# The opening of a two-layer decoder kernel: gain row spread by TensorE, fused scaling on VectorE, loads in halves, identity transposes first

## The chip, the cores and the metric

The kernel runs on one core of one Trainium2 chip. The time is the device time of one execution in microseconds (us). A core has TensorE (PE in the profile; PEld is its weight load), VectorE (DVE), ScalarE (ACT), GpSimd (POOL) and SyncE (SP, which here only issues DMAs). Each engine has its own instruction queue, taken in order; engines wait for each other by semaphores. TensorE writes its results into PSUM, eight banks of 128 x 512 fp32; all else lies in SBUF.

## The reference

Two layers over x of 512 rows by 1024 features, fp32. Layer 0 has dilated-window attention as its mixer, layer 1 a gated linear recurrence; a gated convolutional feed-forward follows each. Every sub-layer stands between two root-mean-square norms. The opening computes the first norm and the first product with the attention weights:

```python
def rms_norm(x, g):
    xf = x.astype(jnp.float32)
    y = xf * lax.rsqrt(jnp.mean(xf * xf, axis=-1, keepdims=True) + RMS_EPS)
    return (y * g.astype(jnp.float32)).astype(x.dtype)

for layer in range(DEPTH):
    h = rms_norm(x, norm_mix_pre[layer])
    h = dilated_attention_mixer(h, attn_w_qkv[j], ...)   # or rglru_mixer; both begin with h @ w
    x = x + rms_norm(h, norm_mix_post[layer])
    h = rms_norm(x, norm_ffn_pre[layer])
    h = conv_ffn(h, ...)
    x = x + rms_norm(h, norm_ffn_post[layer])
```

The kernel makes each of these products of three passes in the format fp32r: a value is split into hi (rounded) and lo (the remainder), and hi x hi, hi x lo and lo x hi are summed in PSUM.

## The kernel before

The 512 rows of x lie as four row tiles of 128 in `x_sb`, 1024 features wide. Weights come from HBM in chunks of 1 MB (`load`, on SP's queue, three `raw` buffers). `pump` takes one unit of a chunk, half of it, and issues the split: per 128 x 512 piece one ScalarE copy to `whi` (L146) and one VectorE subtraction to `wlo` (L147). Eight split units may live. `take` returns a unit for use and pumps if it isn't there yet; `tick`, called between matmul groups, pumps too and runs the side jobs of attention. The order of every engine's queue is the order in which the Python code issues instructions; nothing reorders it.

The opening stands at the end of the kernel function. L951 issues a root on one column, so that ScalarE loads its table. Then come the loads, all on SP: row tile 0 of x (512 KB), the gain row read 128 times into all partitions (`gain`, 512 KB, L142), weight chunk 0, tile 1, chunk 1, tiles 2 and 3.

`first_norm` (L304) is a generator with two steps. The first multiplies each half of a tile by the gain (L312: on VectorE for tile 0, on GpSimd for tiles 1 to 3) and squares and sums each half on ScalarE (L315). The second adds the two sums (L318), makes 1/root with one correction step (L319 to L325: one ScalarE root, the rest on VectorE) and scales the halves (L328 and L331 on VectorE, L330 on ScalarE). `transposed` (L293) brings a scaled tile into the feature-major `hT`: per half four TensorE transposes into a PSUM bank (L297), a ScalarE copy to the hi part (L301), a VectorE subtraction to the lo part (L302).

The first matmul work is `values` (L595) of attention: for each row tile t, 24 matmuls (8 feature blocks, three passes, L246 to L248) of a 128 x 128 block of `hT` with a 512-wide block of weights, into a bank `v`. It calls `start` (L962) through `begin`: before tile 0 it issues the whole norm and transposes of tile 0, the four units of chunks 0 and 1, the whole norm of tile 1 and the first step of tiles 2 and 3; before tile 1 the transposes of tile 1 and the second step of tiles 2 and 3; after tile 1's matmuls the transposes of tiles 2 and 3. The two first results are copied out of PSUM after that (L623).

Behind this, attention goes on with queries and keys of a head pair (`feat_tiles`), and side jobs build the bias tables: for each of three groups a small fp32 matmul (`bv`, L563), a copy, a DMA to HBM (`rowv`, L565), a DMA that copies it 128 times (`skew`, 1.5 MB, L566). The scores of a head (L651) wait for a load from it (`toe`, L579). These three DMAs are on GpSimd's queue.

The main lines are:

```python
(nc.gpsimd if t else nc.vector).tensor_tensor(xs[t][i], xh, halves(g)[i], op=ALU.mult)   # L312
nc.scalar.activation(junk, xh, AF.Square, accum_out=ss[:, c : c + 1])                     # L315
nc.scalar.activation(hi, raw, AF.Copy)                                                    # L146
nc.vector.tensor_tensor(lo, raw, hi.bitcast(F32), op=ALU.subtract)                        # L147
```

Of the kernel before, what the change touches and what calls it, by code (L numbers as in the profile page):

```python
# [18 lines left out]
P = 128  # L19
S = 512  # L20
D = 1024
# [55 lines left out]
def kernel(  # L77
# [42 lines left out]
    def nm(s):  # L120
        uid[0] += 1
        return f"{s}{uid[0]}"
# [7 lines left out]
    def small(cols, s="s"):  # L130
        return sp.tile([P, cols], F32, tag=f"s{cols}", name=nm(s))
# [32 lines left out]
    def pump(limit=2):  # L164

        for _ in range(limit):
            i = state["cv"]
            if not pieces and i < state["dma"]:
                pieces.extend((i, j, u) for j, u in enumerate(parts_of(plan[i][0], raws.pop(i))))
                state["cv"] += 1  # L170
            if pieces and state["live"] < W_UNITS:
                i, j, raw = pieces.pop(0)
                hi, lo = (
                    wp.tile([P] + list(raw.shape[1:]), F32R, tag=t, name=nm("w" + t)) for t in ("hi", "lo")
                )
# [66 lines left out]
    def w_rows(w, r0):  # L242
        plan.append(("rows", 2, D, [(w[r0 : r0 + 256, :].rearrange("(k p) c -> p k c", p=P), 2)]))

    def mm3(dst, l, r, start, stop):
        mm(dst, l[0], r[0], start=start, stop=False)  # L246
        mm(dst, l[0], r[1], start=False, stop=False)  # L247
        mm(dst, l[1], r[0], start=False, stop=stop)  # L248

    def rms(parts, before=None, after=None):  # L250

# [17 lines left out]
    def root_table():  # L269

        one = small(1)
        nc.scalar.activation(one, ident[:, 0:1], AF.Sqrt)

    def halves(ap):
        return [ap[:, 0:512], ap[:, 512:1024]]

    def new_hT():
        return tuple(htp.tile([P, KD, S], F32R, tag=f"hT{i}", name=nm(f"hT{i}")) for i in range(2))
# [11 lines left out]
        yield wait  # L290
        transposed(t, xs, hT)

    def transposed(t, xs, hT):  # L293
        for i in range(2):
            ps = psum("tr")
            for k in range(4):
                nc.tensor.transpose(ps[:, k * P : (k + 1) * P], xs[i][:, k * P : (k + 1) * P], ident)  # L297
# [3 lines left out]
            nc.scalar.activation(hi, ps3, AF.Copy)  # L301
            nc.vector.tensor_tensor(lo, ps3, hi.bitcast(F32), op=ALU.subtract)  # L302

    def first_norm(tiles, g, scaled):  # L304

        n = len(tiles)
        ss, v, y, q = small(4), small(2), small(2), small(2)
        xs = {t: [gen(s="xs") for _ in range(2)] for t in tiles}
        for i in range(2):
            for j, t in enumerate(tiles):  # L310
                xh = halves(x_sb[:, t, :])[i]
                (nc.gpsimd if t else nc.vector).tensor_tensor(xs[t][i], xh, halves(g)[i], op=ALU.mult)  # L312
                junk = gen(s="junk")
                c = 2 * i + j
                nc.scalar.activation(junk, xh, AF.Square, accum_out=ss[:, c : c + 1])  # L315
        yield
        v, y, q = v[:, :n], y[:, :n], q[:, :n]
        nc.vector.tensor_tensor(v, ss[:, 0:n], ss[:, 2 : 2 + n], op=ALU.add)  # L318
        nc.vector.tensor_scalar(v, v, 1.0 / D, EPS, op0=ALU.mult, op1=ALU.add)  # L319
        nc.scalar.activation(y, v, AF.Sqrt)  # L320
        nc.vector.reciprocal(y, y)
        nc.vector.tensor_tensor(q, y, y, op=ALU.mult)
        nc.vector.tensor_tensor(q, q, v, op=ALU.mult)
        nc.vector.tensor_scalar(q, q, -0.5, 1.5, op0=ALU.mult, op1=ALU.add)
        nc.vector.tensor_tensor(y, y, q, op=ALU.mult)  # L325
        for j, t in enumerate(tiles):
            if t == 1:
                nc.vector.tensor_scalar(xs[t][0], xs[t][0], y[:, j : j + 1], None, op0=ALU.mult)  # L328
            else:
                nc.scalar.activation(xs[t][0], xs[t][0], AF.Copy, scale=y[:, j : j + 1])  # L330
# [213 lines left out]
    def attention(hT, post, pre):  # L544
# [50 lines left out]
        def values(vs, permute, midway=None):  # L595

            if permute:
                vd = dp.tile([S, 512], F32, name=f"vrows{len(vrows)}")
                vrows.append(vd)
            ids = [chunk(), chunk()]  # L600
            banks = {}
            begin = first_tiles[0] if first_tiles else None
            for t in range(4):
                if begin and t < 2:
                    begin(t)
                banks[t] = psum("v")
                for k in range(KD):
                    mm3(
                        banks[t],
                        [h[:, k, t * P : (t + 1) * P] for h in hT],  # L610
                        [v[:, k % 2, :] for v in take(ids[k // 4], k // 2 % 2)],
                        k == 0,
                        k == KD - 1,
                    )
                    if t == 3 and k % 4 == 3:
# [319 lines left out]
    for layer in range(2):  # L935
# [23 lines left out]
    scaled = {}  # L959
    parts = [first_norm(tiles, g, scaled) for tiles in ([0], [1], [2, 3])]  # L960
# [54 lines left out]
```

## Time and profile before

| what | value |
|---|---|
| median of 3 runs | 1498.67 us (1498.09 to 1500.18) |
| the profiled execution | 1498.71 us |
| its span | 1496.9 us |
| mean granted TensorE clock over the span | 0.997 |
| first instruction of TensorE | 10.35 us |
| VectorE's wlo (L147), all 504 of the weights | 328.1 us, 697 ns mean |
| GpSimd's gain products (L312), six | 9.5 us, 1602 ns mean |
| waiting of TensorE for L330 before its first transpose | 10.4 us |

The span is the time from the first to the last instruction in the profile; the execution's time has a little around it. In a timeline or chain a row begins with the start in us from the span's beginning and the length; "x8" merges eight instructions of a line; "out<-in" names the tiles with their buffer numbers left out. A bracket gives how long the engine sat idle before, and what ended that. In the table of groups the two numbers behind the bar are the busy time in us and the mean of one in ns. A matmul's length includes its way through the array, so the rate is read from the distance between starts.

### The profile page before, as it was taken

Reading aid. Unit: us, or ns where it says so; the run is one execution under the profiler, and the core shown is the slowest. Engines: PE = TensorE matmul, PEld = TensorE weight load, DVE = VectorE, ACT = ScalarE, POOL = GpSimd, SP = SyncE. Lnnn points to the kernel's source line nnn. Section 1 sums busy time; section 2 is a strip of 40 time slices with the busy share of each in tenths; the row PEclk is TensorE's granted clock in tenths of the full one; section 3 lists DMA queues with packets and bytes.
Section 4 is the critical chain, followed back from the end, with each engine's and each line's share of the span. In section 5 each row is a group of like instructions: output and inputs, shape, how many; then the busy total and the mean of one; then the engine's idle time right before and its main releaser. Section 6 shows DMA issues by size and latency. Waiting matters only on the chain.

```text
span 1496.9 us, 18111 instructions
## 1 busy us (share of the span) xinstructions
PE 1474.0 (98%) x7083; PEld 1237.8 (83%) x7083; DVE 795.3 (53%) x1612; ACT 633.7 (42%) x1287; POOL 43.7 (3%) x73
## 2 busy tenths in 40 slices
PE   6999999999999999999999999999999999999998
PEld 4788888888888898888888888988898888888886
DVE  6434334343434586555555336877876555565333
ACT  5334333333334554333344334579554333344321
POOL 3111000000000000000000000000000000000000
PEclk9999999999999999999999999999999999999999
DMA  6543222423334233323233231342233232323301
GB/s 215 184 164 98 92 88 85 133 100 125 107 121 137 95 110 119 106 87 111 85 113 113 85 113 43 99 142 84 85 99 113 92 105 87 110 85 116 109 1 56
DMA packets 116101, 157.64 MB, mean 105 GB/s; under 512 B 5087, under 2 KB 97463, under 8 KB 116016
## 3 DMA queue, kind: packets, MB, share of 16 engines
q1 hardware_dynamic: 111120, 145.24, 29.3%
q0 software_dynamic: 4896, 11.26, 2.3%
q8 instruction: 55, 0.90, 0.3%
q14 instruction: 30, 0.25, 0.0%
HBM read 150.14 MB, written 11.05 MB: 108 GB/s over the span
## 4 chain that ended last, share of the span: by engine, by line
PE 88%; ACT 5%; DVE 4%; DMA 2%; issue 1%; SPq 0%; POOL 0%; DVEq 0%; ACTq 0%; POOLq 0%
PE ps L246 17%; PE ps L248 17%; PE ps L247 17%; PE acc L248 7%; PE acc L246 7%; PE acc L247 7%; PE v L246 3%; PE v L247 3%; PE v L248 3%; DVE wlo L147 2%; DVE xb L838 1%; ACT whi L146 1%; PE S L714 1%; PE tr L297 1%; PE O L772 1%; PE O L699 1%
## 5 line engine op out<-in xcount | busy, mean ns | idle before, releaser
L246 PE MATMUL ps<-hT,whi 128*128 128x512 f32 (+1 forms) x1376 | 518.5, 377 | 0.0
L248 PE MATMUL ps<-hT,wlo 128*128 128x512 f32 (+1 forms) x1376 | 515.2, 374 | 0.0
L247 PE MATMUL ps<-hT,whi 128*128 128x512 f32 (+1 forms) x1376 | 515.1, 374 | 0.0
L147 DVE TENSOR_TENSOR wlo<-raw,whi 128x512 fp32r<-128x512 f32 x504 | 328.1, 697 | 270.3 <-ACT whi L146 270.1
L146 ACT ACTIVATE whi<-raw 128x512 fp32r<-128x512 f32 x504 | 285.2, 623 | 135.0 <-PE acc L248 120.9
L246 PEld LDWEIGHTS ps<-hT,whi 128*128 128x128 f32 x1376 | 259.1, 188 | 47.0 <-ACT qk L590 0.6
L248 PEld LDWEIGHTS ps<-hT,wlo 128*128 128x128 f32 x1376 | 259.0, 188 | 46.5
L247 PEld LDWEIGHTS ps<-hT,whi 128*128 128x128 f32 x1376 | 259.1, 188 | 45.6
L517 DVE SCALAR_TENSOR_TENSOR u<-ps,cols,u 128x511 f32<-128x511 f32 x192 | 143.8, 749 | 140.4 <-ACT u L513 137.0
L248 PE MATMUL acc<-whi,alo 128*128 128x512 f32 x512 | 199.4, 389 | 1.0 <-DVE alo L147 1.0
L246 PE MATMUL acc<-whi,ahi 128*128 128x512 f32 x512 | 200.0, 391 | 0.0
L247 PE MATMUL acc<-wlo,ahi 128*128 128x512 f32 x512 | 199.2, 389 | 0.0
L513 ACT ACTIVATE u<-ps,cols 128x512 f32<-128x512 f32 x96 | 74.8, 780 | 209.9 <-PE ps L248 209.9
L248 PEld LDWEIGHTS acc<-whi,alo 128*128 128x128 f32 x512 | 96.1, 188 | 21.4 <-DVE alo L147 1.4
L246 PEld LDWEIGHTS acc<-whi,ahi 128*128 128x128 f32 x512 | 96.1, 188 | 19.7
L247 PEld LDWEIGHTS acc<-wlo,ahi 128*128 128x128 f32 x512 | 96.1, 188 | 19.6
L246 PE MATMUL v<-whi,hT 128*128 128x512 f32 x192 | 78.3, 408 | 0.0
L247 PE MATMUL v<-wlo,hT 128*128 128x512 f32 x192 | 76.5, 398 | 1.4 <-DVE wlo L147 1.4
L248 PE MATMUL v<-whi,hT 128*128 128x512 f32 x192 | 76.3, 398 | 0.5 <-DVE hT L302 0.5
L528 ACT ACTIVATE u<-u 128x512 f32<-128x512 f32 x48 | 30.3, 632 | 80.6 <-DVE u L517 80.6
L651 DVE CUSTOM_DVE_ANT_0 L<-S,toe 128x128 f32<-128x128 f32 (+1 forms) x96 | 25.2, 320 | 53.4 <-DMA toe<-skew 22.7
L590 ACT ACTIVATE qk<-ps 128x512 f32<-128x512 f32 x24 | 14.3, 597 | 88.7 <-PE ps L248 76.9
(169 smaller groups left out, 1028.5 us busy)
## 6 DMA issues: line engine op xcount, KB each, us to landing
raw<-in_ffn_w_up_dram SPq DMA_DIRECT2D x48, 1024.0 KB, 5.2
raw<-in_attn_w_qkv_dram SPq DMA_DIRECT2D x28, 1024.0 KB, 5.1
raw<-in_ffn_w_down_dram SPq DMA_DIRECT2D x24, 1024.0 KB, 4.9
raw<-in_attn_w_qkv_dram SPq DMA_DIRECT2D x16, 512.0 KB, 4.9
raw<-in_lru_w_in_dram SPq DMA_DIRECT2D x8, 1024.0 KB, 5.4
skew<-rowv POOLq DMA_DIRECT2D x3, 1536.0 KB, 12.3
vrows<-v SPq DMA_DIRECT2D x16, 256.0 KB, 2.8
vp<-vrows SPq DMA_DIRECT2D x16, 256.0 KB, 4.0
```

Of the source, the lines that this page charges most:

```text
L146: nc.scalar.activation(hi, raw, AF.Copy)
L147: nc.vector.tensor_tensor(lo, raw, hi.bitcast(F32), op=ALU.subtract)
L246: mm(dst, l[0], r[0], start=start, stop=False)
L247: mm(dst, l[0], r[1], start=False, stop=False)
L248: mm(dst, l[1], r[0], start=False, stop=stop)
L297: nc.tensor.transpose(ps[:, k * P : (k + 1) * P], xs[i][:, k * P : (k + 1) * P], ident)
L513: nc.scalar.activation(u, ps, AF.Identity, scale=cc[:, j : j + 1], bias=cc[:, 48 + j : 49 + j])
L517: nc.vector.scalar_tensor_tensor(u[:, d:], ps[:, : S - d], wc, u[:, d:], op0=ALU.mult, op1=ALU.add)
L528: nc.scalar.activation(u, u, AF.Gelu_apprx_tanh)
L651: nc.vector.tensor_tensor_reduce(dst, ps, bias, scale=1.0, scalar=3 * NEG, op0=ALU.add, op1=ALU.max, accum_out=mx)
L699: mm(po[:, a * P : (a + 1) * P], pts[a, j], vtile(v, a - 1 + j, h % 4), start=j == js[0], stop=j == 1)
L714: mm(ps[:, c], q[hh][:, c], k[hh][:, c], start=True, stop=True)
```

## The change

The gain row is no longer read 128 times by a DMA. The new `first_gain` loads it into one partition (two DMAs of 2 KB on ScalarE's queue), multiplies it on TensorE by a column of ones (K = 1, fp32) into two PSUM banks and copies these to `g` on VectorE. Twelve transposes of the identity into an unused bank stand before and twelve after these two matmuls.

Row tile 0 of x and chunks 0 and 1 are loaded in two halves each; the SP order is tile 0, chunk 0, tile 1, chunk 1, tiles 2 and 3. The root for the table is issued after `first_gain`.

`first_norm` no longer multiplies by the gain on its own: a fused VectorE instruction per half computes x times the scale times the gain, for all tiles. The second half of tile 0 is squared and summed on VectorE. In `start`, tile 1's second step and tiles 2 and 3's first step move from before tile 0's matmuls to before tile 1's; the second step of tiles 2 and 3 moves to after tile 1's matmuls. The four weight units are interleaved differently with tile 0's transposes and tile 1's squares.

In `values`, tile 0's six matmuls of a unit are sorted by pass (hi x hi of both blocks first). For all other tiles the order is as before.

```diff
+WARM = 12
...
-            nc.sync.dma_start(raw[:, :, at : at + n] if kind == "value" else raw[:, at : at + n, :], src)
+            if i < 2:
+                for k in (0, 2):
+                    nc.sync.dma_start(raw[:, k : k + 2, :], src[:, k : k + 2, :])
+            else:
+                nc.sync.dma_start(raw[:, :, at : at + n] if kind == "value" else raw[:, at : at + n, :], src)
...
-    def transposed(t, xs, hT):
-        for i in range(2):
+    def transposed(t, xs, hT, parts=(0, 1)):
+        for i in parts:
...
-    def first_norm(tiles, g, scaled):
+    def first_norm(tiles, g):
...
-        for i in range(2):
-            for j, t in enumerate(tiles):
-                xh = halves(x_sb[:, t, :])[i]
-                (nc.gpsimd if t else nc.vector).tensor_tensor(xs[t][i], xh, halves(g)[i], op=ALU.mult)
+        for j, t in enumerate(tiles):
+            for i, h in enumerate(halves(x_sb[:, t, :])):
+                acc = (ss, s1)[i][:, j : j + 1]
                 junk = gen(s="junk")
-                c = 2 * i + j
-                nc.scalar.activation(junk, xh, AF.Square, accum_out=ss[:, c : c + 1])
-        yield
+                if t == 0 and i:
+                    nc.vector.tensor_tensor_reduce(
+                        junk, h, h, scale=1.0, scalar=0.0, op0=ALU.mult, op1=ALU.add, accum_out=acc
+                    )
+                else:
+                    nc.scalar.activation(junk, h, AF.Square, accum_out=acc)
+        nc.vector.tensor_scalar(b, ss, 1.0 / D, EPS, op0=ALU.mult, op1=ALU.add)
+        yield xs
+        nc.vector.scalar_tensor_tensor(v, s1, 1.0 / D, b, op0=ALU.mult, op1=ALU.add)
         nc.scalar.activation(y, v, AF.Sqrt)
...
         for j, t in enumerate(tiles):
-            if t == 1:
-                nc.vector.tensor_scalar(xs[t][0], xs[t][0], y[:, j : j + 1], None, op0=ALU.mult)
-            else:
-                nc.scalar.activation(xs[t][0], xs[t][0], AF.Copy, scale=y[:, j : j + 1])
-            nc.vector.tensor_scalar(xs[t][1], xs[t][1], y[:, j : j + 1], None, op0=ALU.mult)
-        scaled.update(xs)
+            for i, h in enumerate(halves(x_sb[:, t, :])):
+                nc.vector.scalar_tensor_tensor(
+                    xs[t][i], h, y[:, j : j + 1], halves(g)[i], op0=ALU.mult, op1=ALU.mult
+                )
+        yield xs
...
+                for u in range(4):
+                    W = take(ids[u // 2], u % 2)
+                    steps = [(k, a, b) for k in (2 * u, 2 * u + 1) for a, b in PASSES]
+                    if begin and t == 0:
+                        steps.sort(key=lambda s: PASSES.index(s[1:]))
...
+    def first_gain(src):
+
+        g = cp.tile([P, D], F32, tag="gain", name=nm("gain"), bufs=2)
+        row = [gen(s="row") for _ in range(2)]
+        for r, h in zip(row, halves(src)):
+            nc.scalar.dma_start(r[0:1, :], h)
+        one = gen(s="one")
+        nc.vector.memset(one[0:1, :P], 1.0)
+        warm = psum("warm")
+        for _ in range(WARM):
+            nc.tensor.transpose(warm[:, :P], ident, ident)
+        for r, h in zip(row, halves(g)):
+            ps = psum("gain")
+            mm(ps, one[0:1, :P], r[0:1, :], start=True, stop=True)
+            nc.vector.tensor_copy(h, ps)
+        for _ in range(WARM):
+            nc.tensor.transpose(warm[:, :P], ident, ident)
+        return g
+
+    hT = new_hT()
+    for i in range(2):
+        c = slice(i * 512, (i + 1) * 512)
+        nc.sync.dma_start(x_sb[:, 0, c], x[0, 0:P, c])
+    g = first_gain(norm_mix_pre[0:1, :])
     root_table()
-    hT = new_hT()
-    nc.sync.dma_start(x_sb[:, 0, :], x[0, 0:P, :])
-    g = gain(norm_mix_pre, 0, nc.sync)
+    load()
     for t in range(1, 4):
-        if t < 3:
+        nc.sync.dma_start(x_sb[:, t, :], x[0, t * P : (t + 1) * P, :])
+        if t == 1:
             load()
-        nc.sync.dma_start(x_sb[:, t, :], x[0, t * P : (t + 1) * P, :])
...
         if t == 0:
-            for _ in parts[0]:
-                pass
+            next(norm_of[0])
+            xs = next(norm_of[0])
             pump(1)
-            transposed(0, scaled[0], hT)
+            transposed(0, xs[0], hT, (0,))
             pump(1)
-            pump(2)
-            for _ in parts[1]:
-                pass
-            next(parts[2])
+            transposed(0, xs[0], hT, (1,))
+            pump(1)
+            next(norm_of[1])
+            pump(1)
         elif t == 1:
-            transposed(1, scaled[1], hT)
-            next(parts[2], None)
+            transposed(1, next(norm_of[1])[1], hT)
+            next(norm_of[2])
         else:
-            transposed(2, scaled[2], hT)
-            transposed(3, scaled[3], hT)
+            xs = next(norm_of[2])
+            transposed(2, xs[2], hT)
+            transposed(3, xs[3], hT)
```

More of the change, by code (lines that the diff above doesn't have):

```diff
@@ L243, in w_rows @@
         plan.append(("rows", 2, D, [(w[r0 : r0 + 256, :].rearrange("(k p) c -> p k c", p=P), 2)]))
+    PASSES = [(0, 0), (0, 1), (1, 0)]
     def mm3(dst, l, r, start, stop):
-        mm(dst, l[0], r[0], start=start, stop=False)
-        mm(dst, l[0], r[1], start=False, stop=False)
-        mm(dst, l[1], r[0], start=False, stop=stop)
+        for n, (a, b) in enumerate(PASSES):
+            mm(dst, l[a], r[b], start=start and n == 0, stop=stop and n == 2)
     def rms(parts, before=None, after=None):
@@ L302, in transposed @@
             nc.vector.tensor_tensor(lo, ps3, hi.bitcast(F32), op=ALU.subtract)
[L304 removed]
+    def first_norm(tiles, g):
         n = len(tiles)
[L307 removed]
+        ss, b, v, y, q = (small(2)[:, :n] for _ in range(5))
+        s1 = small(2)[:, :n]
         xs = {t: [gen(s="xs") for _ in range(2)] for t in tiles}
[L309 to L312 removed]
+        for j, t in enumerate(tiles):
+            for i, h in enumerate(halves(x_sb[:, t, :])):
+                acc = (ss, s1)[i][:, j : j + 1]
                 junk = gen(s="junk")
[L314 to L319 removed]
+                if t == 0 and i:
[7 more added lines that the diff above has]
+        nc.vector.scalar_tensor_tensor(v, s1, 1.0 / D, b, op0=ALU.mult, op1=ALU.add)
         nc.scalar.activation(y, v, AF.Sqrt)
         nc.vector.reciprocal(y, y)
[L322 to L323 removed]
+        nc.vector.tensor_tensor(q, y, v, op=ALU.mult)
+        nc.vector.tensor_tensor(q, q, y, op=ALU.mult)
         nc.vector.tensor_scalar(q, q, -0.5, 1.5, op0=ALU.mult, op1=ALU.add)
@@ L606, in values @@
                 banks[t] = psum("v")
[L607 to L615, printed above, removed]
+                for u in range(4):
[3 more added lines that the diff above has]
+                        steps.sort(key=lambda s: PASSES.index(s[1:]))
+                    for k, a, b in steps:
+                        mm(
+                            banks[t],
+                            hT[a][:, k, t * P : (t + 1) * P],
+                            W[b][:, k % 2, :],
+                            start=(k, a, b) == (0, 0, 0),
+                            stop=(k, a, b) == (KD - 1, 1, 0),
+                        )
+                    if t == 3 and u % 2:
                         done(2)
@@ L959 @@
-    scaled = {}
-    parts = [first_norm(tiles, g, scaled) for tiles in ([0], [1], [2, 3])]
+    norm_of = {t: first_norm(tiles, g) for t, tiles in ((0, [0]), (1, [1]), (2, [2, 3]))}
     def start(t):
         if t == 0:
-            for _ in parts[0]:
-                pass
+            next(norm_of[0])
+            xs = next(norm_of[0])
             pump(1)
-            transposed(0, scaled[0], hT)
+            transposed(0, xs[0], hT, (0,))
             pump(1)
-            pump(2)
-            for _ in parts[1]:
-                pass
-            next(parts[2])
+            transposed(0, xs[0], hT, (1,))
+            pump(1)
+            next(norm_of[1])
+            pump(1)
```

## The prediction

> **What bounds the kernel now.** I read the page first.
>
> ```profile
> span 1496.9 us, 18111 instructions
> PE 1474.0 (98%) x7083; PEld 1237.8 (83%) x7083; DVE 795.3 (53%) x1612; ACT 633.7 (42%) x1287; POOL 43.7 (3%) x73
> ```
>
> TensorE is the bound over the span. The change leaves every matmul of the layers in place, so it can win or lose only what TensorE waits, or does at half rate, in the opening. I take as its end the first matmul of row tile 2. The chain of waits (start, length, work, in us) says who sets that time:
>
> ```profile
> 1.19 5.43 DMA gain<-in_norm_mix_pre_dram
> 6.73 1.29 DVE xs L312 x2
> 9.52 0.72 ACT xs L330
> 10.79 2.40 DVE wlo L147 x2
> 14.31 8.04 DVE wlo L147 x6
> 23.93 0.49 DVE xs L328
> 24.46 1.48 PE tr L297 x8
> 73.96 9.89 DMA toe<-skew
> ```
>
> First it is the 512 KB broadcast of the gain row, then VectorE: wlo alone holds the chain for 10.4 us. From 24.46 TensorE holds it. The timeline (start, length, engine, line, work, in brackets the idle time before) shows why wlo is slow:
>
> ```profile
> 11.38 2.94 POOL L312 TENSOR_TENSOR xs<-x_sb,gain 128x512 f32<-128x512 f32 x2 [7.49 <-DMA x_sb<-in_x_dram]
> 15.29 6.52 POOL L312 TENSOR_TENSOR xs<-x_sb,gain 128x512 f32<-128x512 f32 x4 [0.97 <-DMA x_sb<-in_x_dram]
> 36.83 2.50 DVE L147 TENSOR_TENSOR wlo<-raw,whi 128x512 fp32r<-128x512 f32 x4 [0.47 <-ACT whi L146]
> ```
>
> Six wlo take 8.04 us (1.34 each) beside GpSimd's gain products; four take 2.50 (0.62 each) when GpSimd is still. The third view is TensorE's rate, from the timeline and from the busy time by stretch (its PEclk, the granted clock, is the third number from the end):
>
> ```profile
> 14.86 0.63 PE L247 MATMUL v<-wlo,hT 128*128 128x512 f32 x1
> 15.29 0.63 PE L248 MATMUL v<-whi,hT 128*128 128x512 f32 x1
> 29.20 0.39 PE L246 MATMUL v<-whi,hT 128*128 128x512 f32 x1
> 29.43 0.39 PE L247 MATMUL v<-wlo,hT 128*128 128x512 f32 x1
> 25.00:26.00 1.00, 1.00 (x7) 0.71 (x5) 0.19 (x1) 0.80 (x4) 0.00 (x0) 0.52 1.07 380
> ```
>
> A 512-column matmul starts every 0.43 us early on and every 0.23 us later. The granted clock falls to 0.52 again after the gap before 24.46 (for the first matmuls the column has no record, so I go by spacing).
>
> **The change part by part.** I follow four stages; "before" is this profiled execution.
>
> Stage 1, up to the first scaling (9.52 before). Its rows:
>
> ```profile
> 1.03 0.29 POOL masks.py:199 TENSOR_SCALAR_AFFINE_SELECT ident<-ident 128x128 f32<-128x128 f32 x1
> 7.94 0.15 DVE L318 TENSOR_TENSOR s<-s 128x1 f32<-128x1 f32 x1
> 10.38 1.94 PE L297 MATMUL tr<-ident,xs 128*128 128x128 f32 x8 [10.38 <-ACT xs L330]
> 50.83 0.81 PE L563 MATMUL bv<-oh,rb 33*8 33x384 f32 x2
> 51.67 0.55 DVE L564 COPY bv<-bv 8x384 f32<-8x384 f32 x1 [2.53 <-PE bv L563]
> L592 DVE COPY qk<-ps 128x512 f32<-128x512 f32 x24 | 16.6, 691 | 63.0 <-PE ps L248 63.0
> 83.99 0.29 DVE L651 CUSTOM_DVE_ANT_0 L<-S,toe 128x128 f32<-128x128 f32 x1 [13.27 <-DMA toe<-skew]
> 84.20 0.42 DVE L651 CUSTOM_DVE_ANT_0 L<-S,toe 128x256 f32<-128x256 f32 x1
> rb<-in_rel_bias_dram POOLq DMA_DIRECT2D x1, 3.0 KB, 6.3
> DMA to landing us min/median/max: 3.7/10.5/12.4
> ```
>
> The identity is ready at 1.32, so the first 12 transposes can begin at 1.4. At half clock one costs 0.21 (eight took 1.94, of which the last one's own 0.42 is pipeline): 12 x 0.21 = 2.6, to 4.0. The spread itself stands nowhere before. The nearest row is bv, a plain fp32 matmul: two instructions for 384 columns, 0.33 apart at full clock, so 0.43 at 512 columns and 0.85 at half clock. Two halves are four instructions: 3.4 at half clock (to 7.4) or 1.7 at full. About 0.2 passes until VectorE's copy starts, as from the last bv start plus 0.33 to 51.67: 7.6. The copy is 0.69, to 8.3. Then the new squares-and-sum on VectorE, queued behind both copies. The fused reduction costs 0.29 at 128 columns and 0.42 at 256, so about 0.69 at 512 (an estimate from these two): 9.0. From there seven small VectorE instructions and one root, as many as from 7.94 to 9.52: 1.58. First scaling at 10.6, 1.1 **later** than before.
>
> The bounds of that 10.6. If the clock rises as early as 4.2, after a stretch of transposes, the four instructions shrink by 1.6 and it is 9.0. I take the half clock, as before's eight transposes and the two matmuls after them left the rate low. The Trainium skill says the same on its page "TensorE: Matmul & The Clock Gate" (Part 4: PE-mode transpose): transposes do not count as activity for the clock gate. It speaks against 24 of the added instructions; by it stage 1 ends at 10.6, without it near 9.8, and this trace cannot decide. The two row loads are issued on ScalarE's queue at about 0.8 and 1.2. With x_sb's least landing of 3.7 the second is in by 4.9, with rb's 6.3 by 7.5, and 2 KB beside 512 KB should be under the 3.7; past 4.0 every us is a us of delay, so the far end is 14.1. I take 4.0, between, nearer to the small side. The second 12 transposes end at 10.0, under the copies and the root; without that cover they would cost 2.6. The three more general buffers and three more banks are free again before the layers ask for them. The ACT queue's two issues stand ahead of the table load, which is still done long before the root. SP issues nine loads where it issued seven, some 0.9 us later for the last, but 512 KB less travel ahead of it and row tiles 2 and 3 are read only past 23. Halved loads therefore count as nothing: x_sb lands 12.4 after issue at worst, near 17.
>
> Stage 2, first scaling to that of tile 1 (23.93 before).
>
> ```profile
> 11.51 0.60 ACT L301 ACTIVATE hT<-tr 128x512 fp32r<-128x512 f32 x1 [0.23 <-PE tr L297]
> 16.07 0.61 ACT L315 ACTIVATE junk<-x_sb 128x512 f32<-128x512 f32 x1
> 17.20 0.19 ACT L315 ACTIVATION_READ_ACCUMULATOR junk<-x_sb 128x1 f32 x1
> 22.28 0.15 DVE L318 TENSOR_TENSOR s<-s 128x1 f32<-128x1 f32 x1
> 36.13 2.23 ACT L146 ACTIVATE whi<-raw 128x512 fp32r<-128x512 f32 x4
> 515.63 1.42 DVE L344 SCALAR_TENSOR_TENSOR x_sb<-post,s,x_sb 128x512 f32<-128x512 f32 x2
> ```
>
> A fused scaling costs 0.75, two 1.42. So tile 0's first half is ready at 11.35, its transposes start at 11.4, and ScalarE takes them up 1.1 later, as before (10.38 to 11.51): 12.5. ScalarE's list is then hT 0.6, two whi 1.1 (0.55 each, 2.23 for four), hT 0.6, two whi 1.1, tile 1's two squares 1.3 (16.07 to 17.39), two whi 1.1: 18.3. The last wlo ends 0.65 later, 18.95. VectorE's own list from 10.6 is two scalings 1.42, eight wlo at 0.62, two hT remainders of the same form 1.24, one small: 7.8, to 18.4, so ScalarE now leads. Here GpSimd's six products are gone, and with them 8 x 0.7 us of stretched wlo. From 22.28 to 23.93 the tail took 1.65; one of its small instructions (0.18) now stands ahead of the wait, so 1.47: 20.4 instead of 23.93, **3.5 earlier**. The sorted passes of tile 0 save a wait of at most 0.5 on TensorE, which is not what sets tile 1; counted as nothing.
>
> Stage 3. 0.75 for the scaling, then from transposes to first matmul 1.37 as before (24.46 to 25.83): 22.55 instead of 25.83.
>
> Stage 4, to tile 2.
>
> ```profile
> 22.76 0.61 ACT L315 ACTIVATE junk<-x_sb 128x512 f32<-128x512 f32 x1
> 25.12 0.18 ACT L315 ACTIVATION_READ_ACCUMULATOR junk<-x_sb 128x1 f32 x1
> 25.83 0.80 PE L246 MATMUL v<-whi,hT 128*128 128x512 f32 x1
> 25.98 0.60 ACT L301 ACTIVATE hT<-tr 128x512 fp32r<-128x512 f32 x1 [0.20 <-PE tr L297]
> 32.61 1.91 PE L297 MATMUL tr<-ident,xs 128*128 128x128 f32 x16
> 34.27 0.47 PE L246 MATMUL v<-whi,hT 128*128 128x512 f32 x1
> ```
>
> Tile 1's 24 matmuls took 6.8 (25.83 to 32.61) with six or so at half clock; all at full clock they take 24 x 0.227 = 5.45. They end at 29.35 or 28.0. A **new wait** appears: the squares of tiles 2 and 3 now follow tile 1's hT on ScalarE. hT ends 0.75 after the first matmul (26.58 before), 23.3; four squares take 2.54 (22.76 to 25.30), 25.85; the tail 1.5, 27.35; four scalings in a row on VectorE, 0.75 + 3 x 0.67 = 2.76, 30.1 (before, ScalarE did two of them). Behind tile 3's scaling wait its transposes, and behind those on TensorE all of tile 2. The last four transposes cost 0.42 (16 took 1.66): 30.55. With the low clock in tile 1 it is 29.35 + 1.66 = 31.0. Middle 30.8, against 34.27: **3.5 us earlier**. What follows hangs on TensorE's progress and moves along.
>
> The profiled execution took 1498.71, 1.8 of it outside the span, and stands 0.04 above the median of the runs: 1498.71 - 3.5 = 1495.2.
>
> **The rivals.**
> - *Transposes raise the clock.* Stage 1 ends between 9.0 and 10.6, and the first transposes run at full clock (0.4 less). Gain 3.7 to 5.5, middle 4.5: 1494.2. For it: the rate rose at 25.8 to 28.5 in a stretch that began with transposes. Against: the first stretch from 10.38. The rule of the Trainium skill above speaks against it too.
> - *Given back later.* The toe load (73.96 in the chain) is 9.9 us of DMA. If the weight loads that moved forward collide with the 1.5 MB copies behind it, half is lost: 1496.9. For it: VectorE idled 13.27 for it. Against: bv, the copies and the loads are all released by TensorE's progress.
> - *The row is late.* TensorE stands in order behind the spread, VectorE behind its copies. If the 2 KB rows are served like the later x_sb loads, the second lands at 1.2 + 12.4 = 13.6, 9.6 late: 1498.7 - 3.5 + 9.6 = 1504.8. It decides from a landing at 7.5 on (no gain); from 10.5 the kernel is slower by 3.0. For it: rb's 3 KB took 6.3 in this stage. Against: only x_sb's first half is ahead, and x_sb's first load took 3.7. The Trainium skill's page "DMA: Bandwidth & Descriptors" (section on SWDGE, HWDGE and iDMA) has each DMA engine take its queues in turn, which would keep the rows near 3; rb's row does not show that.
>
> **How the numbers follow.** A measurement tells this kernel from no change at about 0.2%, 3.0 us, so below 1495.7 is faster. Forecast 45%, at 1495.2, itself 1494.6 to 1495.9 with a sixth of it short of 3.0. Clock rival 25%, all faster. Given back 20%, nearly all within. Late row 10%: half within, the rest slower; and 2% for what I do not see. Faster 0.38 + 0.25 + 0.01 = 0.64, same 0.29, slower 0.07. The range leaves out the last part of each side: 1493.4 to 1497.8.
>
> **What would show it.** Gain's copies ending near 8.3 and first scaling near 10.6; wlo at 0.62 throughout with no GpSimd product; tile 1's first matmul near 22.5; the last scaling near 30, tile 2 near 30.8; spacing 0.43 at tile 0's first matmuls. Wrong if the row's DMA releases the spread, if wlo stays above 1 us, or if TensorE waits longer than before between 70 and 100.

## The result and the profile after

| | before | after |
|---|---|---|
| median of 6 runs each | 1498.59 us (1498.09 to 1500.18) | 1493.61 us (1492.05 to 1494.06) |
| ratio after/before | | 0.9964, 95% interval 0.9951 to 0.9977 |
| profiled execution, its span | 1498.71, 1496.9 | 1493.31, 1491.5 |

The kernel is faster by 5.0 us by the medians, by 5.4 (3.4 to 7.3) by the ratio. 3.5 were forecast: right in sign, short by a third. By the medians the result stands at the low edge of the range (1493.4 to 1497.8), by the ratio just below it.

The chain of waits after (start, length, work) answers to the chain of before:

```profile
1.38 2.81 PE warm L974 x12
4.19 3.72 PE gain L977 x4
...
10.74 0.76 DVE xs L337
...
15.85 1.22 ACT junk L325 x4
...
20.23 0.76 DVE xs L337
22.39 6.02 PE v L621 x24
28.41 1.36 PE tr L303 x12
...
29.79 0.63 PE tr L303 x4
...
69.62 9.68 DMA toe<-skew
```

No wlo holds it for long now; the spread, ScalarE's list and TensorE follow each other. The timeline of the same kernel has the two ends of the work that the prediction priced, the gain's last copy and the four scalings with what stands behind them:

```profile
7.94 0.69 DVE L978 COPY gain<-gain 128x512 f32<-128x512 f32 x1 [1.01 <-PE gain L977]
8.55 0.68 DVE L321 CUSTOM_DVE_ANT_0 junk<-x_sb 128x512 f32<-128x512 f32 x1
...
26.91 2.74 DVE L337 SCALAR_TENSOR_TENSOR xs<-x_sb,s,gain 128x512 f32<-128x512 f32 x4
...
28.25 2.17 PE L303 MATMUL tr<-ident,xs 128*128 128x128 f32 x16
...
30.18 0.48 PE L621 MATMUL v<-whi,hT 128*128 128x512 f32 x1
```

The table of groups for VectorE from 11.5 to 19 (busy us, mean ns) shows that wlo is no longer stretched:

```profile
L148 DVE TENSOR_TENSOR wlo<-raw,whi 128x512 fp32r<-128x512 f32 x8 | 5.2, 687 | 0.5 <-ACT whi L147 0.5
```

| step (us) | before | forecast | after |
|---|---|---|---|
| first scaling | 9.52 | 10.6 | 10.74 |
| tile 1's scaling | 23.93 | 20.4 | 20.23 |
| tile 1's first matmul | 25.83 | 22.55 | 22.39 |
| last of four scalings ends | | 30.1 | 29.65 |
| tile 2's first matmul | 34.27 | 30.8 | 30.18 |

Up to tile 1 the forecast holds within 0.2. It parts from the run at tile 2: the busy time by stretch (granted clock third from the end) is whole in tile 1 after,

```profile
24.00:28.00 4.00, 4.00 (x19) 3.31 (x18) 2.24 (x9) 1.65 (x7) 0.00 (x0) 1.00 0.02 7
28.00:32.00 4.00, 3.96 (x26) 3.28 (x25) 4.00 (x7) 3.12 (x7) 0.00 (x0) 1.00 0.01 4
```

and was not in the profiled execution of before, nor in another run of that kernel (second fence):

```profile
24.00:28.00 4.00, 3.54 (x13) 2.82 (x14) 2.58 (x7) 2.58 (x8) 0.00 (x0) 0.63 0.70 243
28.00:32.00 4.00, 4.00 (x18) 3.26 (x18) 1.54 (x7) 1.34 (x2) 0.00 (x0) 0.94 0.00 0
```

```profile
24.00:28.00 4.00, 3.50 (x12) 2.94 (x13) 2.36 (x6) 2.53 (x8) 0.00 (x0) 0.50 0.72 248
28.00:32.00 4.00, 4.00 (x13) 3.16 (x13) 1.79 (x8) 1.54 (x3) 0.00 (x0) 0.68 0.00 0
```

The profiled pair differs by 5.4 us of span: 4.09 at tile 2's first matmul (34.27 to 30.18); 0.54 behind VectorE's last row of the chain (4.4 us to the end of the span before, 3.9 after, rows further down); and 0.77 between, of which TensorE's wait for the first scores' probabilities, behind the toe load, has 0.5 (0.8 before, 0.3 after).

### The profile page after: what moved, and what is told of

It is laid out like the page before. It is cut to its first block, busy times and chain, and to the rows that moved or that the text cites. A ratio compares the mean times of both kernels' runs of the same rounds, so it can differ in the third digit from the quotient of the medians.

```text
span 1491.5 us, 18162 instructions
## 1 busy us (share of the span) xinstructions
PE 1480.5 (99%) x7111; PEld 1242.2 (83%) x7111; DVE 794.1 (53%) x1618; ACT 631.7 (42%) x1282; POOL 34.2 (2%) x67
## 4 chain that ended last, share of the span: by engine, by line
PE 90%; ACT 5%; DVE 4%; DMA 1%; issue 1%; POOL 0%; DVEq 0%; ACTq 0%; POOLq 0%
PE ps L254 52%; PE acc L254 23%; PE v L621 8%; DVE wlo L148 1%; ACT whi L147 1%; DVE xb L851 1%; PE tr L303 1%; PE O L785 1%; PE S L727 1%; PE O L712 1%; DMA toe<-skew 1%; ACT sig L872 1%; PE S L677 1%; PE PT L766 0%; ACT sig L891 0%
## 5 line engine op out<-in xcount | busy, mean ns | idle before, releaser
L254 PE MATMUL ps<-hT,whi 128*128 128x512 f32 (+1 forms) x2752 | 801.9, 376 | 0.0
L254 PEld LDWEIGHTS ps<-hT,whi 128*128 128x128 f32 x2752 | 502.9, 188 | 92.5 <-ACT qk L598 0.6
L148 DVE TENSOR_TENSOR wlo<-raw,whi 128x512 fp32r<-128x512 f32 x504 | 322.8, 687 | 270.2 <-ACT whi L147 270.1
L621 PE MATMUL v<-whi,hT 128*128 128x512 f32 x384 | 124.8, 399 | 0.0
L621 PEld LDWEIGHTS v<-whi,hT 128*128 128x128 f32 x384 | 72.8, 190 | 15.6 <-ACT hT L307 0.5
L600 DVE COPY qk<-ps 128x512 f32<-128x512 f32 x24 | 16.6, 691 | 63.0 <-PE ps L254 63.0
L347 DVE TENSOR_TENSOR post<-acc,gain 128x512 f32<-128x512 f32 x32 | 21.8, 688 | 45.7 <-ACT junk L261 45.7
```

Of the source, the lines that this page charges most:

```text
L254: mm(dst, l[a], r[b], start=start and n == 0, stop=stop and n == 2)
L347: nc.vector.tensor_tensor(u[i], banks[i], gh[i], op=ALU.mult)
L600: nc.vector.tensor_copy(dst, src)
L621: mm(banks[t], hT[a][:, k, t * P : (t + 1) * P], W[b][:, k % 2, :], start=(k, a, b) == (0, 0, 0), stop=(k, a, b) == (KD - 1, 1, 0),)
```

## The experiments

Each comes with the median of its runs (or the time of a single run), and that of the kernel before on the same chip. A single run has one time and one profile; the expectations call it a look.

**Both kernels again.** No edit.

> The changed kernel again. Theory J (the 1.3 us gained behind the opening is scatter of DMA landings that the chain crosses: the toe load, the last value rows, the last output): tile 2's first matmul again at 30.2 +- 0.5, but the stretch from there to the end scatters by about 1 us from run to run, and the median gain over before is 4 to 5 us. Rival S (the earlier start shortens these waits for good): the stretch from tile 2's first matmul to the end is again about 1.3 us shorter than before's, and the gain stays above 5.

> The kernel before again, for a second trace. Theory J: tile 2's first matmul at 34.3 +- 0.7 (0.6 of it by whether tile 1 meets the half clock), the toe landing and the last value rows differ from the first trace by some tenths. Rival S: both waits as in the first trace within 0.1.

1493.48 (1492.41 to 1493.68; ratio 0.9963, 0.9950 to 0.9975) against 1498.71; the single run of before took 1498.74. In the changed kernel tile 1 is again at full clock throughout. In the kernel before, tile 2's first matmul came at 35.35, 1.1 later than in the first profile and outside the range expected, with tile 1 at half clock for twice as long. TensorE's wait behind the toe load is now 0.8 in the changed kernel and none in the kernel before, so the 0.5 that the profiled pair has there is scatter, as theory J says; the gain stays at 5.2 all the same.

**GpSimd's products back.** For tiles 1 to 3 the gain is multiplied on GpSimd again and VectorE only scales.

```diff
                 acc = (ss, s1)[i][:, j : j + 1]
+                if t:
+                    nc.gpsimd.tensor_tensor(xs[t][i], h, halves(g)[i], op=ALU.mult)
...
+                if t:
+                    nc.vector.tensor_scalar(xs[t][i], xs[t][i], y[:, j : j + 1], None, op0=ALU.mult)
+                    continue
```

> The changed kernel with tiles 1 to 3 multiplied by the gain on GpSimd again, and scaled on VectorE by a plain multiply. Theory P (the gain of the change is VectorE freed from GpSimd's products): the products run from about 11 to 14 and 16 to 23, wlo beside them takes 1.2 to 1.8 instead of 0.65, tile 1's scaling comes about 3 us later and the time is about 1496.3. Rival O (the gain is the new order of norms, splits and transposes): wlo's wait is hidden, time within 0.7 of the changed kernel's.

1497.88 (1496.69 to 1498.92), ratio 0.9994 (0.9985 to 1.0003): 4.4 above the changed kernel, more than expected, and no longer distinct from before. The groups of VectorE from 11.5 to 24, then GpSimd's timeline:

```profile
L148 DVE TENSOR_TENSOR wlo<-raw,whi 128x512 fp32r<-128x512 f32 x8 | 9.3, 1206 | 0.0
L342 DVE SCALAR_TENSOR_TENSOR xs<-x_sb,s,gain 128x512 f32<-128x512 f32 x1 | 1.8, 1762 | 0.0
```

```profile
15.04 6.61 POOL L320 TENSOR_TENSOR xs<-x_sb,gain 128x512 f32<-128x512 f32 x4 [0.75 <-DMA x_sb<-in_x_dram]
```

Eight wlo take 9.3 us, not 5.2, and one fused scaling beside GpSimd 1.76, not 0.75; tile 1's scaling comes at 24.84. Stage 2's mechanism is shown, and it carries nearly the whole gain.

**The fused scaling alone.** The kernel before, with its broadcast gain, whole loads and old order; only the gain products go.

```diff
-                (nc.gpsimd if t else nc.vector).tensor_tensor(xs[t][i], xh, halves(g)[i], op=ALU.mult)
...
+            for i, h in enumerate(halves(x_sb[:, t, :])):
+                nc.vector.scalar_tensor_tensor(
+                    xs[t][i], h, y[:, j : j + 1], halves(g)[i], op0=ALU.mult, op1=ALU.mult
+                )
```

> The kernel before with one edit: no gain product ahead of the scaling, each half scaled and multiplied by the gain in one fused VectorE instruction (no GpSimd product); loads, broadcast, order as before. Theory P (VectorE freed of GpSimd is the gain, the TensorE spread only delays): first scaling near 7.5 instead of 9.5, wlo at 0.65, bounded by the landing of weight chunk 1 near 13.4; tile 1's first matmul near 20.7, tile 2's near 27.6, time about 1491.5, that is 2 us better than the whole change. Rival N (the parts of the change are needed together): no better than 1493.5.

1492.67 (1492.45 to 1493.68), ratio 0.9960 (0.9946 to 0.9974): this one edit gives as much as the whole change. Its chain and the timeline row of tile 2's first matmul:

```profile
2.68 11.46 DMA raw<-in_attn_w_qkv_dram
14.17 2.19 ACT whi L146 x4
16.36 1.24 ACT junk L314 x4
19.20 0.77 DVE xs L327
```

```profile
28.88 0.48 PE L246 MATMUL v<-whi,hT 128*128 128x512 f32 x1
```

The bound is now the landing of chunk 1 at 14.14, later than the 13.4 expected, and the time is 1.2 above what was expected. Tile 2 starts 1.3 sooner than in the changed kernel.

**The other parts, one at a time.** First no transposes of the identity (`WARM = 0`):

> The changed kernel without its 24 identity transposes. Theory C (transposes and the K = 1 spread do not raise TensorE's clock; the first twelve only keep the spread waiting, since the rows land at 2.1 and 3.1): the spread runs from 2.2 to 5.6 instead of 4.1 to 7.8, first scaling near 8.6 instead of 10.7, everything behind 2.1 earlier, about 1491.3. Rival H (they keep the clock up for the first real work): the first real matmuls stay at half clock longer, the time is the same or up to 2 us longer.

1492.23 (1491.81 to 1492.69), ratio 0.9956 (0.9944 to 0.9969): 1.25 **below** the changed kernel. The timeline row of the spread, then the chain:

```profile
2.17 3.75 PE L977 MATMUL gain<-row,one 1*128 1x512 f32 x4 [2.17 <-DMA row<-in_norm_mix_pre_dram]
```

```profile
3.15 10.03 DMA raw<-in_attn_w_qkv_dram
13.20 1.15 ACT whi L147 x2
...
18.73 0.76 DVE xs L337
```

The spread starts at 2.17, not 4.12, and runs without a break, so the second row was in by 3.9. The 2.0 won is cut to 1.5 at tile 1's scaling, since chunk 1's first half lands only at 13.18. The transposes cost 1.25 us by the medians as they stand, and 1.5 at tile 2's first matmul (28.67).

Second, the changed kernel with the gain broadcast by SP's DMA in place of rows, spread and transposes (`g = gain(norm_mix_pre, 0, nc.sync)`):

> The changed kernel with the 512 KB broadcast of the gain row by SP's DMA in place of rows, spread, copies and transposes. Theory P: the gain is in near 6.7, first scaling near 6.8, but the weight halves land 1.3 later (chunk 1's first half near 13.5 to 14.5), so tile 1's scaling comes near 19 instead of 20.2: about 1492.2. Rival (the spread pays by freeing the DMAs): 1493.5 or more.

1494.33 (1493.16 to 1494.88), ratio 0.9967 (0.9956 to 0.9979), 2.1 above the kernel without transposes; it has none either. Its chain:

```profile
3.62 11.79 DMA raw<-in_attn_w_qkv_dram
...
20.97 0.76 DVE xs L337
```

The broadcast gain lands at 9.34, not near 6.7, and the first scaling comes at 9.48, against 8.74 without transposes. But the chain passes through chunk 1. The 512 KB move the landing of its first half from 13.18 to 15.41, and there the spread's worth lies. The fused scaling alone also reads the gain by broadcast, in the old order with whole loads, and has tile 1's scaling at 19.20, not 20.97: beside a broadcast, the new order and the halved loads together did not pay.

Third, no transposes, the tile 0 norm ahead of the gain copies, and tile 0 scaled straight from the two PSUM banks of the spread:

```diff
+                if t == 0:
+                    nc.vector.scalar_tensor_tensor(xs[t][i], g_ps[i], y[:, j : j + 1], h, op0=ALU.mult, op1=ALU.mult)
```

> The changed kernel without the identity transposes, with tile 0's whole norm ahead of the gain's copies on VectorE and tile 0 scaled straight from the PSUM banks of the spread. Theory W (past the spread the next bound is the landing of chunk 1): first scaling near 6.7, but tile 1's scaling near 18.7 as without the transposes, time within 0.5 of 1492.2. Rival (the spread is still the bound): tile 1's scaling near 16.8, 1490.3.

1493.02 (1492.13 to 1494.64), ratio 0.9962 (0.9949 to 0.9975). Its chain:

```profile
3.15 9.60 DMA raw<-in_attn_w_qkv_dram
...
18.50 0.76 DVE xs L340
```

The first scaling comes at 6.68, tile 1's hardly sooner than without transposes alone (18.73): chunk 1's landing holds it, at 12.75 here, as theory W has it. The median is 0.8 above the 1492.2 expected, with runs scattered over 2.5.

Fourth, whole loads in the changed kernel, and fifth, tile 0's passes unsorted, in a single run and then in five:

> The changed kernel with tile 0 of x and chunks 0 and 1 loaded whole. Theory P: ScalarE comes to chunk 0 at 9.6 and to chunk 1 at 14.7, after they land even whole, so tile 2's first matmul stays at 30.2 +- 0.3. Rival (halves pay): later by up to 1.

> The changed kernel with tile 0's passes in the old order. Theory P: TensorE waits up to 0.5 more in tile 0, but tile 1's scaling, on VectorE, stays at 20.2 and tile 2's first matmul at 30.2 +- 0.2. Rival: later by 0.5 or more.

> The changed kernel with tile 0's passes in the old order, timed in rounds. Theory L (the early clock of the single look was the phase of a window): median within 0.5 of the changed kernel's 1493.5, tile 2's first matmul near 30.2 unless the clock is up by 5 again. Rival (the old pass order is better): median near 1492 with the clock up only near 16.

Whole loads took 1493.64, as the changed kernel, and the five runs without sorting 1493.35 (1491.86 to 1493.59; ratio 0.9962, 0.9948 to 0.9975). Tile 2's first matmul comes at 29.72 and 29.70, 0.5 sooner than in the changed kernel, for a reason that neither edit is about: in these two traces the granted clock rises at 10.9 and 10.8, behind the second twelve transposes, and in the chain tile 0's first four transposes take 0.67, not 1.13. Neither the halves nor the order of passes is seen to count in the opening.

With whole loads the end of the span differs: the chains' last rows of before, of whole loads (then its page's first line), and of after:

```profile
1492.49 0.66 DVEq L1011
```

```profile
1487.48 0.66 DVEq L1044
```

```profile
span 1491.8 us, 18156 instructions
```

```profile
1487.63 0.66 DVEq L1046
```

From there to the end of the span are 4.4, 4.3 and 3.9. From the last matmul's start to the end it is 7.77 to 7.85 in every trace of a kernel with whole loads (before, the kernels made from it, this one) and 7.25 to 7.32 in every one with halved loads. The traces show where this lies. Behind the last store SyncE waits for the DMAs' semaphores one after the other, in ten waits, and the last store's semaphore stands at another place among them. The waits that end behind that store's landing are eight before, seven with whole loads and four after; from the landing to the end of the span are 1.72, 1.65 and 1.09. That two or three loads more give the last store another semaphore is the likely reason; it was not tried apart.

The single run without sorting took 1491.89. It had a quicker clock early; its timeline:

```profile
4.12 2.19 PE L977 MATMUL gain<-row,one 1*128 1x512 f32 x4
```

This is 2.19 for the spread, against 3.78 in the same view of the changed kernel. Here the first twelve transposes raised the clock, at 4.6, and the first scaling came at 9.15, not 10.74. The clock fell again for 3.41 at 11.4.

**Can transposes raise the clock?** The second twelve become 40 transposes, or 20 plain fp32 products of the identity (40 instructions); both lie in an unused bank.

```diff
-        for _ in range(WARM):
-            nc.tensor.transpose(warm[:, :P], ident, ident)
+        for _ in range(40):
+            nc.tensor.transpose(warm[:, :P], ident, ident)
```

> The changed kernel with 40 identity transposes instead of 12 behind the spread, the partner of the run with 40 product instructions. Theory C (transposes do not count for the clock): spacing 0.21 to the end at 16.4, although a whole 3.4 us stretch holds nothing but transposes; the first real matmuls at half clock; tile 0 late by 4.8, tile 2's first matmul near 35. Rival H: spacing falls to 0.11 between 10 and 15, as it did with products.

> The changed kernel with the second twelve transposes replaced by 20 plain fp32 products of the identity with itself (40 instructions, all 128 rows, no transpose mode). Theory C (only real matmuls over the whole array count for the clock): their spacing goes from 0.21 to 0.11 somewhere between 10.3 and 14.7, and tile 0's transposes and first matmuls run at full clock. Rival K (nothing this short or this early raises it): spacing 0.21 throughout, to 16.4. The time is 1 to 4 us above the changed kernel's, as the products delay tile 0.

They took 1497.81 and 1499.01, in single runs, some 4.3 and 5.5 above the changed kernel. The group itself is 4.5 and 3.9 us longer, and tile 2 starts 2.9 and 2.3 later; the rest is lost behind the toe load, where TensorE waits 1.9 and 2.2, and with products the clock then falls once more, for 3.41. TensorE's timeline with 40 transposes, then after:

```profile
7.83 7.33 PE L980 MATMUL warm<-ident 128*128 128x128 f32 x40
15.00 1.04 PE L303 MATMUL tr<-ident,xs 128*128 128x128 f32 x8
```

```profile
7.83 2.82 PE L980 MATMUL warm<-ident 128*128 128x128 f32 x12
...
11.54 1.97 PE L303 MATMUL tr<-ident,xs 128*128 128x128 f32 x8 [0.89 <-DVE xs L337]
```

Twelve take 2.82 at half clock (0.42 of it the last one's way through), 0.218 apart; 40 at that pace would take 39 x 0.218 + 0.42 = 8.9, and took 7.33, and the eight behind them 1.04, not 1.97. No product had come between: transposes count. In the single starts the spacing changes from 0.21 to 0.11 at 13.5 (12.0 with products), and the granted clock on record rises at the same times.

**Clock in tile 1 alone.** The kernel before, with twelve identity transposes in TensorE's gap ahead of tile 1's:

```diff
         elif t == 1:
+            fill = psum("fill")
+            for _ in range(12):
+                nc.tensor.transpose(fill[:, :P], ident, ident)
             transposed(1, scaled[1], hT)
```

> The kernel before with twelve identity transposes in TensorE's gap ahead of tile 1's transposes. Theory D (the low clock in tile 1 was part of before's time, and transposes count for the clock): the clock stays up from tile 0 on, tile 1's 24 matmuls take 5.5 to 6.0 instead of 6.8 to 7.7, tile 2's first matmul comes at 33.0 to 33.5 instead of 34.3 to 35.3, and the time falls by 1.0 to 2.0. Rival (transposes do not hold the clock, or the gap is no matter): same time within 0.4, or slower by the transposes.

> The bridged kernel again. Theory D: the late value rows of the first look were chance; tile 2's first matmul near 33.4 again, no drop of the clock near 500, a look at 1497.0 to 1498.2 and a median 0.5 to 1.5 below before's. Rival G (given back): the look again loses 1 or more at the toe load or the value rows, and the median is again that of before within 0.4.

> A third look at the kernel before. Theory D: TensorE's clock drops ahead of tile 1 again for one or two stretches of 3.4, tile 2's first matmul between 34.2 and 35.4. Rival: no drop in this look, tile 2 near 33.4.

> A third look at the bridged kernel, with the same expectations: theory D 1497.0 to 1498.2 with nothing lost behind the opening, rival G a loss of 1 or more at one of the two DMA waits.

> A fourth look at the kernel before, with the same expectations: a drop and tile 2 between 34.2 and 35.4, or by the rival none and tile 2 near 33.4.

11 runs took 1498.93 against 1498.57 (ratio 1.0003, 0.9994 to 1.0011), 11 more 1498.64 against 1498.79 (1.0001, 0.9992 to 1.0010); single runs 1497.95, and 1499.21 and 1499.31 for before. TensorE's timeline of the second bridged trace and of a single run of before, on one chip:

```profile
23.05 1.47 PE L977 MATMUL fill<-ident 128*128 128x128 f32 x12
24.54 1.09 PE L297 MATMUL tr<-ident,xs 128*128 128x128 f32 x8
...
33.43 0.48 PE L246 MATMUL v<-whi,hT 128*128 128x512 f32 x1
...
497.83 0.71 PE L772 MATMUL O<-PT,vp 128*128 128x128 f32 x4 [0.63 <-DMA vp<-vrows]
498.75 0.71 PE L772 MATMUL O<-PT,vp 128*128 128x128 f32 x4 [0.21 <-DMA vp<-vrows]
```

```profile
24.50 1.97 PE L297 MATMUL tr<-ident,xs 128*128 128x128 f32 x8 [1.32 <-DVE xs L328]
...
35.56 0.48 PE L246 MATMUL v<-whi,hT 128*128 128x512 f32 x1
```

The clock holds through tile 1 in all three bridged traces, and tile 2 starts 2.1 sooner here (0.8 to 2.2 against the four traces of before). Yet the time does not fall. TensorE waits for the value rows (`vp`, a load of attention) near 497 for 1.5, 0.84 and 0.40 in the three bridged traces and in none of the four of before; in the first the clock then falls for 3.41 as well. Why it waits there only in the bridged kernel stays open, and so does the rest of what is given back. The edit also takes one more PSUM bank, which shifts the banks of all that follows; that was not tried apart.

**A version meant to beat both.** No transposes; the spread's banks serve tiles 0 and 1; the norms of tiles 1, 2 and 3 are issued one after the other ahead of where they are needed, and tile 3's transposes move into tile 2's matmuls.

```diff
-        elif t == 1:
-            transposed(1, next(norm_of[1])[1], hT)
-            next(norm_of[2])
+        elif t == 1:
+            transposed(1, later[1], hT)
+            next(norm_of[2])
+            later.update(next(norm_of[2]))
...
+                    if begin and t == 2 and u == 1:
+                        begin(3)
```

> A version meant to beat both: no transposes, tiles 0 and 1 scaled straight from the spread's PSUM banks, tile 1's and tile 2's squares and scales moved ahead, tile 3's transposes in the middle of tile 2's matmuls, tiles 2 and 3 normed singly. Theory W (behind chunk 1's landing near 13 the order of VectorE and ScalarE is the bound): tile 1's scaling right behind the last wlo, near 16.5; tile 1's first matmul near 18.3; tile 2's near 25.2; time about 1489. Rival (the order is not the bound): no better than 1492.

1491.10 (1490.51 to 1491.44) against 1498.63, ratio 0.9951 (0.9937 to 0.9965): 7.5 below before, 2.4 below the changed kernel, and 2 short of what was expected. Its chain and TensorE's timeline:

```profile
13.13 2.08 ACT whi L146 x4
...
16.52 1.32 DVE xs L339 x2
```

```profile
26.16 0.49 PE L623 MATMUL v<-whi,hT 128*128 128x512 f32 x1 [0.25 <-ACT hT L306]
...
29.45 1.03 PE L302 MATMUL tr<-ident,xs 128*128 128x128 f32 x8
```

Tile 2 starts 4.0 sooner than in the changed kernel; tile 3's transposes, now within tile 2, take part of it back.

## Why the prediction was right in part, and where it failed

*Stage 1 held, in part by luck.* 10.74 against 10.6. The spread ran right behind the transposes at half clock, as taken, and so did tile 0's first matmuls (full clock from 16 to 17). But in the single run without sorting the same twenty-four transposes brought 9.15.

*Stage 2 held and carries the gain.* 20.23 against 20.4; wlo 0.65 each (5.2 for eight) against the 0.62 to 0.65 used. GpSimd's products put back undo it.

*Stage 4 failed, in its size.* "With the low clock in tile 1 it is 29.35 + 1.66 = 31.0. Middle 30.8": half of the loss was charged to the changed kernel on the strength of before's single profile. The rows of that profile showed the cause, a gap of TensorE ahead of tile 1, and stage 2 took away most of that gap; the step should have carried this on to the clock. Neither trace of the changed kernel has a drop there. Full clock gives the prediction's own 30.55, and tile 2 started at 30.18. The *new wait* came out as a near tie: the last scaling ended at 29.65, not 30.1, and the last four transposes began at 29.79, a wait that the profile puts down to the transposes ahead of them. By the chain after, TensorE itself holds the time from 22.39 on.

*The same row misled on the side of before.* Tile 2's first matmul came at 34.27 in the profile read, and at 35.35, 35.56 and 35.58 in three more traces, because the half clock around tile 1 lasted 3.41 us in the first and 6.83 in the others. The Trainium skill, page "TensorE: Matmul & The Clock Gate" (Part 1: The HAM clock gate), says that the gate's window runs free of the kernel, so that one kernel's share of slow matmuls changes from run to run; these four traces agree. That the profiled execution still stood at the median is a chance sum: lightest in the clock, longest in the wait behind the toe load (0.8 against 0.3, 0.3 and none).

*The sum with these in.* Over the four traces of before the mean is 35.2, so tile 2 comes 5.0 sooner, not 3.5. From tile 2's first to the last matmul the four take 1454.82, 1453.79, 1454.02 and 1454.13, mean 1454.2; the two after 1454.06 and 1454.49, mean 1454.3. With 0.55 at the end that makes 5.4 to 5.5; measured 5.0 and 5.2 by medians, 5.4 by the ratio. This is an account of traces; the one experiment on the clock alone, in the kernel before, did not bring its part to the end. So the 0.9 that before's row was short of that mean is not shown to be part of the time; that cause stays open.

*Halved loads "count as nothing"*: right in the opening, wrong at the end of the span, by some 0.5, in SyncE's last waits. Sorted passes: nothing, as said.

*The rivals.* "Transposes raise the clock" has a true mechanism. Both traces of the changed kernel ran stage 1 at half clock, but the one run without sorting had the rise and its 9.15 lies in this rival's span. The rule of the Trainium skill that was set against it, on the page named above (Part 4: PE-mode transpose), does not agree with the 40 transposes. Stage 1's number came out for another reason: twelve last 2.8 us, and it is a matter of timing whether they raise the clock. "Given back later": no, by the stretch from tile 2 on. "Row late": no, 3.9 at the latest without the transposes, and in the changed kernel no row's DMA releases the spread.

## What to carry to other kernels

A GpSimd product beside VectorE's two-input products can cost more on VectorE than it spares: fold it into an instruction that VectorE has to run anyway, and look at that edit alone before building more around it. Whether an edit shortens a gap of TensorE should be asked of the clock too, and the share of half clock should be read from several profiles, since one execution may be its lightest. Warming transposes ahead of work that waits in order behind them cost more than they brought: twenty-four cost 1.25 us here by the medians, and the group of forty, which did raise the clock, 4.3 more in a single run.

## What was not expected of the hardware

- Transposes of the identity raise the granted clock once they last long enough: forty did. Twelve (2.8 us) did so in three of the six traces that have both groups of twelve (single run without sorting, profile of the five, whole loads), and not in the two of the changed kernel or with GpSimd's products back. The lengths of half and full clock around tile 1 are 3.41, 6.83 and 10.24, so the gate seems to judge stretches of 3.41. Counted back from the recorded rise, the stretch ahead of it was filled by identity transposes to 81 to 83% in those three traces, while stretches of 78% and less did not raise the clock. In the kernel before one of 86%, transposes and products together, did not either; how full a stretch must be stays open.
- The spread's products of one row appear to count for less. With whole loads, and in the profile of the five unsorted runs, they fill 97 and 94% of a stretch from about 4.0 to 7.4, and the clock rose only one stretch later. Whether they count in part stays open.
- A fused VectorE instruction beside GpSimd takes 1.76 instead of 0.75, wlo up to 1.77 instead of 0.69. The Trainium skill, page "SBUF — State Buffer" (section "SBUF: two separate sides"), has the two engines lock a shared pair of ports for a whole instruction; the lengths here agree.
- With halved first loads the span ends some 0.5 sooner behind its last matmul, more than a millisecond later, because fewer of SyncE's last waits stand behind the last store's landing.
